# The sample units' last product with pairs of V heads as its stationary operand

## The chip, the cores and the metric

The kernel runs on one core of one Trainium2 chip. The metric is the device time of one execution in microseconds. A profile of one further execution, taken by the hardware profiler, shows what each engine did: PE is the matrix engine (PEld its loads of the stationary operand), DVE the vector engine, ACT the scalar engine, POOL GpSimd, SP the engine that issues most DMAs.

## What is computed

The reference is one inference step of a streaming encoder of two layers (width 1024, 16 heads of 64, 4 K/V heads, MLP of 4096), for a prompt of 1024 new frames and for 8 running streams ("sample") of 16 new frames each, which attend to 128 cached positions beside their own. Layer 0 has windowed attention with a distance penalty and sinks, layer 1 chunked attention with a learned bias; K and V of layer 1 come from a projection of the residual after layer 0. The part that the change touches is the sample attention, in both layers:

```python
def attend(q, k, v, bias, sink):
    qg = q.reshape(b, tq, N_KV_HEADS, GROUP, HEAD_DIM)
    s = jnp.einsum('bqhgd,bkhd->bhgqk', qg, k).astype(jnp.float32) * (HEAD_DIM ** -0.5)
    s = s + bias.reshape(N_KV_HEADS, GROUP, tq, -1)
    # softmax over keys, in layer 0 with the sink in its denominator -> p
    o = jnp.einsum('bhgqk,bkhd->bqhgd', p.astype(v.dtype), v)
    return o.reshape(b, tq, N_HEADS * HEAD_DIM)

k_all = jnp.concatenate([cache_k_a[i], ks_], axis=1)   # cache (8, 128, 4, 64), new (8, 16, 4, 64)
v_all = jnp.concatenate([cache_v_a[i], vs_], axis=1)
as_ = attend(qs, k_all, v_all, alibi_bias(pos_s, kpos_a, slopes), sink_a[i])
```

## The kernel before

Tokens are tiles of 128: eight of the prompt and one that holds all 8 x 16 sample tokens. Each layer is a phase of attention (about 25 to 400 us of the span in layer 0, 1130 to 1605 in layer 1), the output projection, the MLP's up part and its down part. Most products take fp32 data split in a high and a low part of type fp32r and are three products of 128x128 by 512 (lines 250 to 252, 205 to 207, 800 to 802).

In the attention phase, a loop over 16 pairs of steps does the prompt's attention, for one tile and one K/V head at a time: scores (L423, L475), softmax, transposes of the probabilities (L362), their split (`pth` by ACT at L154, `ptl` by DVE at L160), the product with V (L370 and L371, called from `V` in `attention`). Other work is put between these steps by tables (`at`, `shift`, `plan`): projections of later tiles, the output projection, and the steps of one *sample unit* at a time.

A sample unit (function `unit`, 16 in each layer) takes one K/V head `j` and two of the 8 streams (`bp`): 4 query heads x 2 streams x 16 tokens are its 128 rows. It is a generator with four places at which other work comes between. It

- loads the cached K (`kc`) and V (`vc`) of that head and those two streams, 128 positions each, and the queries (`qu`) by DMAs that SP issues;
- makes K's split and its transpose (L622, `ps_utr`, copied to `kb` by ACT at L623) and the scores (L627, `ps_us`);
- makes the softmax with ACT and DVE, with the normalized probabilities in `p` and those of the new tokens in `pn`;
- transposes them in three 128x128 pieces (L652 to L654, `ps_utp`), which ACT copies to `pts` (L656);
- makes the last product (L660 to L662): stationary are `vc` for each of the two streams and then `v8`, the new tokens' V, 64 columns each; moving is `pts`, 128 columns. All are plain fp32, not fp32r;
- copies the result's blocks to `so` with two ACT copies (L665) and stores it (L666).

The pool of the unit's tiles has one buffer for each, so the next unit's `vc` is loaded when this one's product is done. The result tile `ps_uo` comes from the PSUM tag `g`, shared with the transposes and the products with V.

The order of instructions on each engine is not the order of the code: the framework's planner simulates a timeline with costs of its own, takes ranks into account (tables `rank`, `rank_s` and so on, and `WO_PRIO`), and writes a fixed order for each engine at build time. An instruction of another shape has another cost in that simulation, and the order around it can come out differently.

Of the kernel before, what the change touches and what calls it, by code (L numbers as in the profile page):

```python
# [10 lines left out]
F32 = mybir.dt.float32  # L11
# [7 lines left out]
P = 128  # L19
# [8 lines left out]
HD = 64  # L28
# [92 lines left out]
class Build:  # L121
# [461 lines left out]
    @ranked_steps  # L583
    def unit(self, up, small, layer, bp, j, v8, gq8, cache_k, cache_v):
        nc = self.nc
        kc = up.tile([P, 2, HD], F32, tag="kc", name="kc")
        nc.sync.dma_start(kc, cache_k[2 * bp : 2 * bp + 2, :, j, :].rearrange("b k d -> k b d"))
        vc = up.tile([P, 2, HD], F32, tag="vc", name="vc")
        nc.sync.dma_start(vc, cache_v[2 * bp : 2 * bp + 2, :, j, :].rearrange("b k d -> k b d"))
        qu = up.tile([P, 2, P], F32R, tag="qu", name="qu")  # L590
        qd = self.qT8d[layer][j][:, bp * P : bp * P + P]
        nc.sync.dma_start(qu[:, 0].bitcast(F32), qd)
        nc.sync.dma_start(qu[0:64, 1].bitcast(F32), qd[64:128])
        nc.sync.dma_start(qu[64:128, 1].bitcast(F32), qd[0:64])
        kb = up.tile([P, 288], F32R, tag="kb", name="kb")
        nc.sync.dma_start(
            kb[:, 256:288].bitcast(F32), self.kT8d[layer][:, j, bp * 32 : bp * 32 + 32]
        )
        if layer == 0:
            bias = self.cst[:, C_SA : C_SA + 288]  # L600
        else:
            bias = up.tile([P, 288], F32, tag="ub", name="ub")
            nc.sync.dma_start(bias, self.biasSd[j])
        kp = kc
        self.eng("c").tensor_tensor(kp, kc, gq8.unsqueeze(1).to_broadcast([P, 2, HD]), ALU.mult)
        if "p" in self.engs:
            yield
            a, b = slice(0, 64), slice(64, 128)
            pt = self.psum("u", [P, P], "ps_utr")
            nc.tensor.transpose(pt, kp.rearrange("p b d -> p (b d)"), self.ident)  # L610
            self.split(kb[a, 0:P], kb[b, 0:P], pt[a])
            self.split(kb[b, P : 2 * P], kb[a, P : 2 * P], pt[b])
        else:
            ks = up.tile([P, 2, P], F32R, tag="uks", name="uks")
            nc.gpsimd.tensor_copy(ks[:, :, 0:HD], kp)
            self.eng("u").tensor_tensor(
                ks[:, :, HD:P], kp, ks[:, :, 0:HD].bitcast(F32), ALU.subtract
            )
            yield
            pt = self.psum("u", [P, 2, P], "ps_utr")  # L620
            for b in range(2):
                nc.tensor.matmul(pt[:, b, :], ks[:, b, :], self.identr, start=True, stop=True)  # L622
            nc.scalar.copy(kb[:, 0:256], pt.rearrange("p b k -> p (b k)"))  # L623
        yield
        s = self.psum("u", [P, 288], "ps_us")
        for v in range(2):
            nc.tensor.matmul(s, qu[:, v], kb, start=(v == 0), stop=(v == 1))  # L627
        mn = small.tile([P, 1], F32, tag="smn", name="smn")
        pn = up.tile([P, P], F32, tag="pn", name="pn")
        nc.gpsimd.memset(pn, 0.0)  # L630
        p = up.tile([P, 288], F32, tag="sp", name="sp") if layer == 0 else bias
        l = small.tile([P, 1], F32, tag="sl", name="sl")
        if layer == 0:
            nc.vector.tensor_tensor_reduce(
                s, s, bias, 1.0, self.susink[:, j : j + 1], ALU.add, ALU.min, mn
            )
            nm = small.tile([P, 1], F32, tag="snm", name="snm")
            nc.vector.tensor_tensor(nm, mn, self.cst[:, C_SLS + j : C_SLS + j + 1], ALU.mult)
            nc.scalar.activation(
                p, s, AF.Exp, bias=nm, scale=self.nslope[:, j : j + 1], accum_out=l  # L640
            )
            li = self.sink_norm(small, nm, self.ssink[:, j : j + 1], l, 1)
        else:
            nc.vector.tensor_tensor_reduce(s, s, bias, 1.0, BIG, ALU.add, ALU.min, mn)
            nc.scalar.activation(p, s, AF.Exp, bias=mn, scale=-1.0, accum_out=l)
            li = small.tile([P, 1], F32, tag="sli", name="sli")
            self.mark = nc.vector.reciprocal(li, l)
        nc.scalar.activation(p[:, 0:256], p[:, 0:256], AF.Copy, scale=li)
        nc.scalar.activation(pn[:, bp * 32 : bp * 32 + 32], p[:, 256:288], AF.Copy, scale=li)
        yield  # L650
        pt2 = self.psum("u", [P, 3, P], "ps_utp")
        nc.tensor.transpose(pt2[:, 0, :], p[:, 0:128], self.ident)  # L652
        nc.tensor.transpose(pt2[:, 1, :], p[:, 128:256], self.ident)
        nc.tensor.transpose(pt2[:, 2, :], pn, self.ident)  # L654
        pts = up.tile([P, 3, P], F32, tag="pts", name="pts")
        nc.scalar.copy(pts, pt2)  # L656
        yield
        po = self.psum("u", [64, 2, 2, 32], "ps_uo")
        pof = po.rearrange("p a b q -> p (a b q)")
        nc.tensor.matmul(pof, vc[:, 0, :], pts[:, 0, :], start=True, stop=False)  # L660
        nc.tensor.matmul(pof, vc[:, 1, :], pts[:, 1, :], start=False, stop=False)
        nc.tensor.matmul(pof, v8[:, j * HD : j * HD + HD], pts[:, 2, :], start=False, stop=True)  # L662
        so = up.tile([P, 2, 32], F32, tag="so", name="so")
        for par in range(2):
            nc.scalar.copy(so[par * 64 : par * 64 + 64], po[:, :, par, :])  # L665
        nc.sync.dma_start(  # L666
            self.oTd[layer][j // 2][ST][:, 0, 2 * (j % 2) : 2 * (j % 2) + 2, bp * 32 : bp * 32 + 32], so
        )
# [1364 lines left out]
```

## Time and profile before

| | |
|---|---|
| median of 3 runs | 2330.3 us (2327.54 to 2332.09) |
| the profiled execution | 2332.31 us, span 2330.5 us |
| granted clock of the matrix engine, mean | 0.993 |
| instructions on PE | 11429 products, as many loads |
| the unit's last products | 192 of them (32 units x 3 x 2 passes) |
| the unit's V loads | 32, 64 KB each |

In the profile's rows, a product reads "128*64 128x128": 128 rows by 64 columns of the stationary operand, then the moving data, 128 partitions by 128 elements. A product's end is modelled, and records of products that follow each other overlap; so the distance from start to start says what one costs, rather than its length. "idle before" is the time in which the engine (PEld: the load) had nothing running ahead of the instruction, with the names of those whose end released it.

### The profile page before, as it was taken

How to read it: one execution, taken by the hardware profiler on the slowest of the kernel's cores; microseconds unless marked ns; L12 is line 12 of the kernel's file. 1: busy time of each engine (PE TensorE's matmuls, PEld its weight loads, DVE VectorE, ACT ScalarE, POOL GpSimd, SP SyncE). 2: the span in 40 equal slices, each digit the busy share in tenths (PEclk: the TensorE clock that was granted, in tenths of full speed). 3: DMA queues.
4: the chain of work that ended last, by engine and by line, in shares of the span. 5: the costliest groups of instructions: out<-in, count | busy, mean ns of one | idle time of the engine just before them, and what ended most of it. 6: DMA issues, size and time to landing. Idle time of an engine off the chain costs nothing.

```text
span 2330.5 us, 33408 instructions
## 1 busy us (share of the span) xinstructions
PE 2273.0 (98%) x11429; PEld 1899.7 (82%) x11429; DVE 1705.2 (73%) x3072; ACT 1330.4 (57%) x2684; POOL 635.5 (27%) x952
## 2 busy tenths in 40 slices
PE   8999999999999999999999999998999999999999
PEld 6787877888888888788788788887888888888887
DVE  6878776856656587898678877777665665778987
ACT  3777665655555555444377666665655555565443
POOL 4333332322222211002443434344222132110011
PEclk9999999999999999999999999999999999999999
DMA  7335566244433688548744656555244343977567
GB/s 274 115 113 160 170 196 204 101 135 145 146 126 127 215 233 196 203 146 199 220 150 115 189 164 182 172 170 176 95 142 139 122 155 113 285 206 197 181 165 199
DMA packets 226219, 392.70 MB, mean 169 GB/s; under 512 B 51592, under 2 KB 125776, under 8 KB 225936
## 3 DMA queue, kind: packets, MB, share of 16 engines
q1 hardware_dynamic: 188320, 283.58, 38.2%
q0 software_dynamic: 36432, 102.26, 16.1%
q10 hardware_dynamic: 1296, 4.72, 0.5%
q8 instruction: 90, 1.47, 0.3%
q14 instruction: 81, 0.66, 0.1%
HBM read 237.10 MB, written 157.15 MB: 169 GB/s over the span
## 4 chain that ended last, share of the span: by engine, by line
PE 83%; DVE 7%; DMA 5%; ACT 3%; issue 1%; SPq 0%; POOL 0%; ACTq 0%; DVEq 0%; POOLq 0%
PE ps_c L800 8%; PE ps_c L801 8%; PE ps_c L802 8%; PE ps_x L800 5%; PE ps_x L802 5%; PE ps_x L801 5%; PE ps_mm L250 4%; PE ps_mm L252 4%; PE ps_mm L251 4%; PE ps_y L802 2%; PE ps_y L801 2%; PE ps_y L800 2%; PE ps_tr L362 2%; PE ps_mm L205 2%; PE ps_mm L206 2%; PE ps_mm L207 2%
## 5 line engine op out<-in xcount | busy, mean ns | idle before, releaser
L800 PE MATMUL ps_c<-w,a 128*128 128x512 f32 x960 | 374.0, 390 | 3.0 <-ACT o L1236 2.0
L801 PE MATMUL ps_c<-w,a 128*128 128x512 f32 x960 | 373.7, 389 | 0.8 <-DVE w L160 0.8
L802 PE MATMUL ps_c<-w,a 128*128 128x512 f32 x960 | 373.5, 389 | 0.0
L988 POOL DMA_DIRECT2D hd<-h x272 | 148.8, 550 | 573.3 <-ACT h L890 377.3
L800 PEld LDWEIGHTS ps_c<-w,a 128*128 128x128 f32 x960 | 180.2, 188 | 42.4 <-ACT o L1236 3.3
L801 PEld LDWEIGHTS ps_c<-w,a 128*128 128x128 f32 x960 | 180.2, 188 | 38.5 <-DVE w L160 1.5
L802 PEld LDWEIGHTS ps_c<-w,a 128*128 128x128 f32 x960 | 180.2, 188 | 37.5
L154 ACT CAST a<-a 128x1536 fp32r<-128x1536 f32 x80 | 118.7, 1483 | 153.2 <-DMA a<-hd 153.0
L250 PE MATMUL ps_mm<-w,hh 128*128 128x512 f32 x432 | 174.4, 405 | 12.1 <-ACT hh L154 5.3
L252 PE MATMUL ps_mm<-w,hl 128*128 128x512 f32 x432 | 173.5, 402 | 1.9 <-DVE hl L160 1.9
L251 PE MATMUL ps_mm<-w,hh 128*128 128x512 f32 x432 | 172.3, 399 | 0.1
L160 DVE TENSOR_TENSOR a<-a 128x1536 fp32r<-128x1536 f32 x80 | 140.2, 1752 | 35.1 <-ACT a L154 34.8
L154 ACT CAST w<-ru 128x512 fp32r<-128x512 f32 (+1 forms) x160 | 110.0, 708 | 89.6 <-PE ps_y L801 32.0
L800 PE MATMUL ps_x<-sx,w 128*128 128x512 f32 (+1 forms) x408 | 158.2, 388 | 0.3 <-ACT w L154 0.3
L154 ACT CAST w<-s 128x2048 fp32r<-128x2048 f32 x56 | 107.1, 1912 | 86.6 <-DVE s L1137 74.9
L802 PE MATMUL ps_x<-sx,w 128*128 128x512 f32 (+1 forms) x408 | 154.8, 379 | 0.9 <-DVE w L160 0.9
L801 PE MATMUL ps_x<-sx,w 128*128 128x512 f32 (+1 forms) x408 | 154.6, 379 | 0.0
L160 DVE TENSOR_TENSOR w<-s,w 128x2048 fp32r<-128x2048 f32 x56 | 128.2, 2288 | 33.9 <-ACT w L154 33.9
L1253 POOL DMA_DIRECT2D xp<-o x28 | 36.2, 1294 | 407.6 <-ACT o L1236 386.2
L160 DVE TENSOR_TENSOR ptl<-ps_tr,pth 128x512 fp32r<-128x512 f32 x180 | 122.0, 684 | 22.5 <-ACT pth L154 20.5
L160 DVE TENSOR_TENSOR w<-ru,w 128x512 fp32r<-128x512 f32 (+1 forms) x160 | 127.3, 798 | 14.4 <-ACT w L154 14.3
L889 ACT ACTIVATE h<-h 128x512 f32<-128x512 f32 (+1 forms) x102 | 62.0, 607 | 117.8 <-DVE h L940 93.7
(273 smaller groups left out, 6120.8 us busy)
## 6 DMA issues: line engine op xcount, KB each, us to landing
a<-hd SPq DMA_DIRECT2D x80, 768.0 KB, 5.5
hd<-h POOLq DMA_DIRECT2D x272, 192.0 KB, 2.5
ru<-in_w_up SPq DMA_DIRECT2D x64, 512.0 KB, 3.8
r<-in_w_down SPq DMA_DIRECT2D x32, 1024.0 KB, 9.6
xp<-o POOLq DMA_DIRECT2D x28, 768.0 KB, 9.5
o<-oTd SPq DMA_DIRECT2D x50, 256.0 KB, 4.0
x<-xp SPq DMA_DIRECT2D x23, 512.0 KB, 5.4
xp<-xo SPq DMA_DIRECT2D x18, 512.0 KB, 3.1
```

The source lines that it names most:

```text
L154: a = nc.scalar.copy(hi, src)
L160: return a, e.tensor_tensor(lo, src, hi.bitcast(F32), ALU.subtract)
L205: nc.tensor.matmul(ps, oh[:, k, :], w[:, 0, k, nn], start=(k == 0), stop=False)
L206: nc.tensor.matmul(ps, oh[:, k, :], w[:, 1, k, nn], start=False, stop=False)
L250: nc.tensor.matmul(ps, a, w[:, 0, k, :], start=(k == 0), stop=False)
L251: nc.tensor.matmul(ps, a, w[:, 1, k, :], start=False, stop=False)
L252: self.lp = nc.tensor.matmul(ps, b, w[:, 0, k, :], start=False, stop=(k == KC - 1))
L800: a = mm(ps, ah, bh, start=first, stop=False, skip_group_check=True)
L801: mm(ps, ah, bl, start=False, stop=False, skip_group_check=True)
L802: return a, mm(ps, al, bh, start=False, stop=last, skip_group_check=True)
L889: a = nc.scalar.activation(t, src, AF.Relu)
L988: return lambda p, z: self.nc.gpsimd.dma_start(self.hd[c // 4][:, p, c % 4], z)
```

## The change

The cached V is loaded for the pair of heads that `j` belongs to (heads 0 and 1, or 2 and 3), so `vc` has 128 columns for each stream instead of 64, and the load brings 128 KB instead of 64. The three products take all 128 columns, and `v8` likewise those of the pair. The result has 128 partitions instead of 64: the lower 64 for the pair's first head and the upper 64 for its second. The two copies read only the half that belongs to `j`; the other half is not used. The number of instructions is the same.

```diff
-        vc = up.tile([P, 2, HD], F32, tag="vc", name="vc")
-        nc.sync.dma_start(vc, cache_v[2 * bp : 2 * bp + 2, :, j, :].rearrange("b k d -> k b d"))
+        jj = slice(j // 2 * 2, j // 2 * 2 + 2)
+        vc = up.tile([P, 2, 2, HD], F32, tag="vc", name="vc")
+        nc.sync.dma_start(vc, cache_v[2 * bp : 2 * bp + 2, :, jj, :].rearrange("b k j d -> k b j d"))
...
-        po = self.psum("u", [64, 2, 2, 32], "ps_uo")
+        po = self.psum("u", [P, 2, 2, 32], "ps_uo")
         pof = po.rearrange("p a b q -> p (a b q)")
-        nc.tensor.matmul(pof, vc[:, 0, :], pts[:, 0, :], start=True, stop=False)
-        nc.tensor.matmul(pof, vc[:, 1, :], pts[:, 1, :], start=False, stop=False)
-        nc.tensor.matmul(pof, v8[:, j * HD : j * HD + HD], pts[:, 2, :], start=False, stop=True)
+        v2 = v8.rearrange("p (j d) -> p j d", d=HD)
+        nc.tensor.matmul(pof, vc[:, 0], pts[:, 0, :], start=True, stop=False)
+        nc.tensor.matmul(pof, vc[:, 1], pts[:, 1, :], start=False, stop=False)
+        nc.tensor.matmul(pof, v2[:, jj], pts[:, 2, :], start=False, stop=True)
+        own = slice(j % 2 * HD, j % 2 * HD + HD)
         so = up.tile([P, 2, 32], F32, tag="so", name="so")
         for par in range(2):
-            nc.scalar.copy(so[par * 64 : par * 64 + 64], po[:, :, par, :])
+            nc.scalar.copy(so[par * 64 : par * 64 + 64], po[own, :, par, :])
```

Lines behind the edit have numbers that are 1 to 3 higher in the changed kernel (L660 becomes L662, L652 becomes L653).

In most places the order stays and only the shape differs. On PE, around the unit's product at about 1495 us of the span (layer 1; `ps_pv` is the prompt's product with V, `ps_tr` a transpose of its probabilities, `ps_sf` scores), before:

```order
L362 MATMUL ps_tr<-identr,p 128x128 x4
L370 MATMUL ps_pv<-pth,VS 128x512
L660 MATMUL ps_uo<-pts,vc 64x128
L661 MATMUL ps_uo<-pts,vc 64x128
L371 MATMUL ps_pv<-ptl,VS 128x512
L662 MATMUL ps_uo<-pts,v_11164 64x128
L362 MATMUL ps_tr<-identr,p 128x128 x4
L475 MATMUL ps_sf<-KT,qT 128x384 x4
```

and now:

```order
L362 MATMUL ps_tr<-identr,p 128x128 x4
L370 MATMUL ps_pv<-pth,VS 128x512
L662 MATMUL ps_uo<-pts,vc 128x128
L663 MATMUL ps_uo<-pts,vc 128x128
L371 MATMUL ps_pv<-ptl,VS 128x512
L664 MATMUL ps_uo<-pts,v_11164 128x128
L362 MATMUL ps_tr<-identr,p 128x128 x4
L475 MATMUL ps_sf<-KT,qT 128x384 x4
```

Nothing moved there: the same product L371 still stands between the second and the third product of the unit, and the three rows of the unit have 128 columns.

Between about 184 and 243 us, in layer 0, the order differs on PE, ACT, DVE and POOL. PE around a unit's scores (`ps_us`) at about 206 us, before (the products L250 to L252 go on for some 25 rows from here; `ps_q` transposes queries):

```order
L370 MATMUL ps_pv<-pth,VS 128x512
L622 MATMUL ps_utr<-identr,uks 128x128 x2
L295 MATMUL ps_q<-identr,qr 128x128 x4
L627 MATMUL ps_us<-kb,qu 128x288 x2
L250 MATMUL ps_mm<-w,hh 128x512
L251 MATMUL ps_mm<-w,hh 128x512
L252 MATMUL ps_mm<-w,hl 128x512
```

and now:

```order
L370 MATMUL ps_pv<-pth,VS 128x512
L623 MATMUL ps_utr<-identr,uks 128x128 x2
L295 MATMUL ps_q<-identr,qr 128x128 x4
L628 MATMUL ps_us<-kb,qu 128x288 x2
L371 MATMUL ps_pv<-ptl,VS 128x512
L370 MATMUL ps_pv<-pth,VS 128x512
L362 MATMUL ps_tr<-identr,p 128x128 x4
L250 MATMUL ps_mm<-w,hh 128x512
L251 MATMUL ps_mm<-w,hh 128x512
```

Two products with V (L371, L370) and four transposes (L362) now stand right behind the unit's scores; before, they came behind the products L250 to L252.

ACT at the same place (`oh` is the high part of an attention output that a DMA brought, `kb` the unit's K, `so` the result of the unit before), before:

```order
L154 CAST w<-raw 128x1024
L665 COPY so<-ps_uo 64x64 x2
L154 CAST pth<-ps_tr 128x512 x2
L154 CAST oh<-o 128x512
L623 CAST kb<-ps_utr 128x256
L261 COPY qr<-ps_mm 128x512
L154 CAST qT<-ps_q 64x4x128
L438 ACTIVATE p,l<-ps_s,nm 128x256 x2
```

and now:

```order
L154 CAST w<-raw 128x1024
L668 COPY so<-ps_uo 64x64 x2
L154 CAST pth<-ps_tr 128x512
L154 CAST oh<-o 128x512
L154 CAST pth<-ps_tr 128x512
L624 CAST kb<-ps_utr 128x256
L438 ACTIVATE p,l<-ps_s,nm 128x256 x2
L261 COPY qr<-ps_mm 128x512
```

Of two casts of `pth`, the second now stands behind `oh`, and two exponentials (L438) come ahead of `qr`. SP's order differs in a few rows at the same time (a query store and a load of `kc` among them). Behind 243 us, PE's order is that of before but for two swaps, of one pair of products with V at about 381 us and of three products in the MLP at about 1646 us.

## The prediction

> **What bounds the kernel now.** I read the page first, then the groups of PE by line and shape, then short timelines around one last product of a sample unit, then the chain of waits.
>
> ```profile
> span 2330.5 us, 33408 instructions
> PE 2273.0 (98%) x11429; PEld 1899.7 (82%) x11429; DVE 1705.2 (73%) x3072; ACT 1330.4 (57%) x2684; POOL 635.5 (27%) x952
> PE 83%; DVE 7%; DMA 5%; ACT 3%; issue 1%; SPq 0%; POOL 0%; ACTq 0%; DVEq 0%; POOLq 0%
> ```
>
> PE sets the pace: 83% of the chain that ended last is PE. A busy share of 98% does not say that PE streams all that time: the records overlap, and stalls shorter than a record are covered by it. So I looked for such stalls in the lines that the change touches.
>
> ```profile
> L660 PE MATMUL ps_uo<-pts,vc 128*64 128x128 f32 x64 | 13.8, 298 | 0.8 <-ACT pts L656 0.8
> L660 PEld LDWEIGHTS ps_uo<-pts,vc 128*64 128x64 f32 x64 | 6.1, 134 | 10.0 <-issue 4.2 <-ACT pts L656 1.2 <-ACT p L438 1.1
> L661 PEld LDWEIGHTS ps_uo<-pts,vc 128*64 128x64 f32 x64 | 7.9, 137 | 0.0
> L423 PEld LDWEIGHTS ps_s<-KT,qT 128*128 128x128 f32 x256 | 36.7, 189 | 6.3 <-ACT p L438 2.6 <-DVE qT L160 0.8 <-ACT qr L261 0.4
> ```
>
> There are 32 units; each product has 64 records, so one fp32 product is two passes, and a unit issues six passes, each with its own load. The first load (L660) has 10.0 us of load idle before it, 0.31 us for each unit, and its named releasers explain little of it. What happens there shows in a timeline (start, length), here of PE around one unit between two 512-wide products, with the loads that begin it and follow it:
>
> ```profile
> 257.17 0.39 PE L207 MATMUL ps_mm<-w,ol 128*128 128x512 f32 x1
> 257.48 0.43 PE L660 MATMUL ps_uo<-pts,vc 128*64 128x128 f32 x2
> 257.75 0.38 PE L661 MATMUL ps_uo<-pts,vc 128*64 128x128 f32 x2
> 257.97 0.38 PE L662 MATMUL ps_uo<-pts,v 128*64 128x128 f32 x2
> 258.28 0.50 PE L370 MATMUL ps_pv<-pth,VS 128*128 128x512 f32 x1
> 258.62 0.39 PE L371 MATMUL ps_pv<-ptl,VS 128*128 128x512 f32 x1
> 257.48 0.19 PEld L660 LDWEIGHTS ps_uo<-pts,vc 128*64 128x64 f32 x2 [0.36 <-ACT p L438]
> 258.28 0.19 PEld L370 LDWEIGHTS ps_pv<-pth,VS 128*128 128x128 f32 x1 [0.17 <-issue]
> ```
>
> And the same neighbours around the three 128-column transposes of a unit:
>
> ```profile
> 1598.28 0.39 PE L370 MATMUL ps_pv<-pth,VS 128*128 128x512 f32 x1
> 1598.51 0.27 PE L652 MATMUL ps_utp<-identr,ub 128*128 128x128 f32 x1
> 1598.62 0.27 PE L653 MATMUL ps_utp<-identr,ub 128*128 128x128 f32 x1
> 1598.72 0.27 PE L654 MATMUL ps_utp<-identr,pn 128*128 128x128 f32 x1
> 1598.75 0.48 PE L371 MATMUL ps_pv<-ptl,VS 128*128 128x512 f32 x1
> 1599.07 0.39 PE L370 MATMUL ps_pv<-pth,VS 128*128 128x512 f32 x1
> 1598.28 0.14 PEld L652 LDWEIGHTS ps_utp<-identr,ub 128*128 128x128 f32 x1
> ```
>
> With 128 columns the load of L652 starts with the product ahead of it (1598.28), and the switch costs nothing: 0.23 us later the transpose runs. With 64 columns the load waits 0.31 us (257.17 to 257.48) until the product ahead is over, and the next 128-column load waits again until L662 is over (0.17 us idle). On both sides of the 64-column group the array runs empty. The rule of the Trainium skill that bears on this is in "TensorEngine Tiling (Array Packing)", Tiling Modes, Key Properties: "Mode switching requires drain". By that rule, whose drain the rows agree with, 128 columns take both stalls away.
>
> **The change part by part.** Removed: the two drains. From the product ahead to the second product behind, the 64-column unit takes 258.62 - 257.17 = 1.45 us. With 128 columns the same stretch is 0.23 (entry, 1598.28 to 1598.51), five steps between six passes, and 0.35 (exit, 1598.72 to 1599.07).
>
> The step. It is 0.108 us between L652 and L654, where a load lasts 0.14 us. A full load that is no transpose lasts 189 ns (L423), and there the step is 0.47/4 = 0.118 us, at 256 columns of moving data:
>
> ```profile
> 93.11 0.64 PE L423 MATMUL ps_s<-KT,qT 128*128 128x256 f32 x4
> 93.58 0.40 PE L252 MATMUL ps_mm<-w,hl 128*128 128x512 f32 x1
> ```
>
> So five steps cost 0.54 to 0.59 us, and a unit 1.12 to 1.17: it saves 0.28 to 0.33 us. I take 0.28, as the plain load of 128 columns is nearest to L423. "TensorE: Matmul & The Clock Gate", LDWEIGHTS (loading the stationary operand), of the Trainium skill speaks against the change: a load takes its columns over 1.2 GHz, so by my estimate from it the 192 loads would grow by 53 ns each, 10.2 us if none were hidden. The rows 137 and 189 ns agree with that growth; that it hides is read from the step above.
>
> Before a transpose the exit is shorter:
>
> ```profile
> 240.75 0.38 PE L662 MATMUL ps_uo<-pts,v 128*64 128x128 f32 x2
> 241.06 0.88 PE L362 MATMUL ps_tr<-identr,p 128*128 128x128 f32 x6
> 1495.09 0.38 PE L661 MATMUL ps_uo<-pts,vc 128*64 128x128 f32 x2
> 1495.40 0.50 PE L371 MATMUL ps_pv<-ptl,VS 128*128 128x512 f32 x1
> 1495.83 0.43 PE L662 MATMUL ps_uo<-pts,v 128*64 128x128 f32 x2
> 1496.19 0.66 PE L362 MATMUL ps_tr<-identr,p 128*128 128x128 f32 x4
> ```
>
> L662 to its successor takes 0.31 us there, in which two passes of 0.108 lie, and the first transpose then waits for its own load; I put the saving at 0.045 us less than above, 0.235 us. By the timelines 13 units are followed by a transpose and 19 by something wider: 19 x 0.28 + 13 x 0.235 = 8.4 us (10.0 us at the short step). In two units, of which the rows from 1495.09 are one, a 512-wide product (L371) stands inside the group, so both drains are paid twice: L661 to L662 takes 0.74 us where 0.22 and a product of 0.23 would be 0.45, some 0.3 each, 0.6 in all. Eight units wait for their data longer than the drain; the entry gains nothing there (0.08 us each, 0.6 in all) and their first load, 52 ns longer, may be bare (0.4). PE's gain: 8.4 + 0.6 - 0.6 = 8.4 us, bounds 8.0 and 10.6.
>
> What of it is on the path: in the chain of waits the product group appears in 25 of the 32 units, the first two and the last of them:
>
> ```profile
> 95.59 0.36 PE ps_uo L660 x2
> 117.85 0.36 PE ps_uo L660 x2
> 1588.48 0.36 PE ps_uo L660 x2
> ```
>
> 8.4 x 25/32 = 6.6 us. The other seven stand where ACT, DVE or a DMA set the time.
>
> Moved: with another shape the planner puts the work of layer 0's attention in another order between about 184 and 243 us; behind that PE's order is the same but for two small swaps. In that stretch the chain of waits leaves PE, and in parts of it the clock was halved, as in the second row:
>
> ```profile
> 178.00:232.00 54.00, 49.67 (x258) 39.71 (x259) 47.14 (x142) 42.80 (x120) 18.16 (x35) 0.94 0.54 161
> 205.40:208.90 3.50, 3.17 (x8) 2.66 (x9) 3.01 (x7) 3.50 (x12) 0.00 (x0) 0.52 0.19 63
> 204.79 0.62 ACT L154 CAST oh<-o 128x512 fp32r<-128x512 f32 x1 [1.95 <-DMA o<-oTd]
> 205.73 0.85 PE L627 MATMUL ps_us<-kb,qu 128*128 128x288 f32 x2 [2.19 <-ACT kb L623]
> ```
>
> (The fields behind the window's length are busy time of PE, PEld, DVE, ACT and POOL, then clock, DMA share, GB/s.) ACT waits 1.95 us for a DMA with oh, its kb stands behind, and PE behind kb. In the new order one of two casts of pth stands behind oh too, and PE asks for it right behind ps_us, ahead of some 25 products that covered it. The cast costs kb about 0.5 us there. On the other side the transposes that stood behind those products come 5 us sooner, which is good for DVE and ACT. A half-clock stretch of 3.5 us costs 1.7 us; one more or one less is possible. I put the reorder at 0, bounds -4 and +4 us.
>
> Added: 64 KB per unit of V that is not used. The load's buffer is free as soon as L661 is done, and it is read a unit later, about 20 us (95.59 to 117.85 for the first two).
>
> ```profile
> vc<-in_cache_v_a SPq DMA_DIRECT2D x16, 64.0 KB, 2.5
> vc<-in_cache_v_b SPq DMA_DIRECT2D x16, 64.0 KB, 3.5
> L665 ACT COPY so<-ps_uo 64x64 f32<-64x64 f32 x64 | 13.1, 205 | 16.1 <-PE ps_uo L662 15.7
> ```
>
> Even twice 3.5 us is covered three times by that; SP issues the same number of transfers. Were the cover gone, a unit would wait up to 3.5 us. The copies on ACT (L665) keep 64x64 elements and only read another half of the partitions: 0.
>
> The sum. The profiled execution took 2332.3 us (span 2330.5, the rest around it), 2.0 above the median of the runs shown. 2332.3 - 6.6 = 2325.7, or **2323.7 us** beside the median.
>
> **The rivals.**
>
> *The drain belongs to the two-pass fp32 product, not to the 64 columns.* In this trace the two cannot be told apart: the only rows with 64 columns are also the only ones with two passes. Against it speaks that inside the group six passes of it follow each other without a drain, and that the transposes, fp32 too, enter and leave freely. Then the drains stay and the bare first load is 52 ns longer, the five steps 0 to 0.045: 32 x 0.052 to 0.097 = 1.7 to 3.1 us on PE, 1.3 to 2.4 on the path: 2332. This would be the case that the change doesn't do what it says.
>
> *PE gains, but the rest takes it back.* DVE, ACT and the DMAs hold 15% of the chain, and DVE is busy 47.14 of 54 us in the stretch from 178. If there the gain before 243 us is lost, and what layer 0 gains behind it waits for DMAs, the 14 units of layer 1 on the chain are left: 14 x 0.26 = 3.6 us, 2326.7, within what can be told from no change.
>
> *The new order stalls.* One mechanism: behind ps_us at about 206 us PE waits for pth and ptl, which ACT makes only after its wait for oh; PE idles, and its clock halves. Price: 2 us a step for the four units up to 243 us, and half clock for three stretches, 8 + 5 = 13 us, less 6.6: 2337. It decides only from 11 us of loss on. Against it: before, the same engines had PE busy in 49.67 of 54 us there.
>
> **How the numbers follow.** My forecast 0.62, the fp32 rival 0.14, the gain taken back 0.17, the stall 0.07. The likeliest case alone spans 2318 to 2328: 10.6 us all on the path with a lucky order below, the order's 4 us above. Range 2317 to 2332, which takes in the two rivals in between and leaves out the stall. A measurement of this kernel tells 0.2%, 4.7 us, from no change: faster means below 2325.6. Faster: 0.80 of the forecast and a third of the gain taken back, 0.55. Same: 0.12 + 0.11 + 0.12 = 0.35. Slower: the stall, a little of the fp32 rival and of a bad order, 0.10.
>
> **What would show it.** The load idle before the first product falls from 10.0 us to under 3, and the timeline shows its load starting with the product ahead: the drain is the columns'. Loads of the group last about 189 ns with steps of 0.11 to 0.12; steps of 0.2 would mean that a full fp32 load does not hide. Layer 1 (1200 to 1605 us), whose order is unchanged, must be some 3 to 4 us shorter; if it is not, the theory of the drain or of the path is wrong. Layer 0's stretch from 178 to 243 us tells what the order did. A longer wait of PE for ptl or kb there would make the prediction wrong on the slow side.

## The result, and the profile after

| | before | after |
|---|---|---|
| median, runs side by side | 2331.61 us (6 runs, 2327.54 to 2336.88) | 2319.99 us (6 runs, 2317.25 to 2324.45) |
| the profiled execution | 2332.31 us, span 2330.5 us | 2321.66 us, span 2319.9 us |

The ratio is 0.9956, with a 95% interval from 0.9944 to 0.9967: between 7.7 and 13.1 us of 2331.6, 10.3 in the middle. The forecast was 6.6 us. Two later comparisons of the same two kernels on other chips (in the experiments) gave 0.9972 and 0.9965, 6.5 and 8.2 us. Over all runs whose granted clock is known one by one the means are 2329.7 us (73 runs of before) and 2322.3 (24 of the change), 7.4 apart. So the change is faster, by 7 to 8 us, and the first comparison stands high.

The page of the changed kernel, in the lines that answer those shown of before (span, busy time of the engines, the chain of waits by engine):

```profile
span 2319.9 us, 33409 instructions
PE 2260.6 (97%) x11429; PEld 1898.7 (82%) x11429; DVE 1707.1 (74%) x3072; ACT 1330.5 (57%) x2684; POOL 634.7 (27%) x952
PE 78%; DMA 7%; DVE 6%; issue 4%; ACT 3%; POOL 1%; SPq 0%; ACTq 0%; DVEq 0%; POOLq 0%
```

PE still sets the pace. PE's busy time fell by 12.4 us, though it executes as many products, and the time of its loads hardly moved, though 192 of them became longer. The groups of the last product by line and shape (count, then busy time and mean ns of one, then the idle time ahead of them):

```profile
L662 PE MATMUL ps_uo<-pts,vc 128*128 128x128 f32 x64 | 12.5, 277 | 1.0 <-ACT pts L657 1.0
L662 PEld LDWEIGHTS ps_uo<-pts,vc 128*128 128x128 f32 x64 | 11.5, 188 | 3.1 <-ACT pts L657 1.4
L663 PEld LDWEIGHTS ps_uo<-pts,vc 128*128 128x128 f32 x64 | 9.7, 192 | 0.0
L664 PEld LDWEIGHTS ps_uo<-pts,v 128*128 128x128 f32 x64 | 9.9, 192 | 0.1
```

The first load's idle time fell from 10.0 to 3.1 us. The loads went from 134 and 137 ns to 188 and 192. The same neighbours as in the prediction's timeline, PE first and then the two loads:

```profile
257.25 0.39 PE L207 MATMUL ps_mm<-w,ol 128*128 128x512 f32 x1
257.48 0.38 PE L662 MATMUL ps_uo<-pts,vc 128*128 128x128 f32 x2
257.70 0.39 PE L663 MATMUL ps_uo<-pts,vc 128*128 128x128 f32 x2
257.92 0.39 PE L664 MATMUL ps_uo<-pts,v 128*128 128x128 f32 x2
258.06 0.48 PE L370 MATMUL ps_pv<-pth,VS 128*128 128x512 f32 x1
258.38 0.39 PE L371 MATMUL ps_pv<-ptl,VS 128*128 128x512 f32 x1
257.25 0.41 PEld L662 LDWEIGHTS ps_uo<-pts,vc 128*128 128x128 f32 x2
258.03 0.19 PEld L370 LDWEIGHTS ps_pv<-pth,VS 128*128 128x128 f32 x1
```

The first load starts with the product ahead of it, at 257.25, and L370's load starts at 258.03, while the unit's last product still runs. The stretch from the product ahead to the second product behind is 258.38 - 257.25 = 1.13 us, where it was 1.45. Passes follow each other at 0.22/2 = 0.11 us (553 ns for five steps), so the longer load hides. And the same view of the changed kernel where a product stands inside the group, and a transpose behind it:

```profile
1485.51 0.47 PE L370 MATMUL ps_pv<-pth,VS 128*128 128x512 f32 x1
1485.83 0.38 PE L662 MATMUL ps_uo<-pts,vc 128*128 128x128 f32 x2
1486.04 0.39 PE L663 MATMUL ps_uo<-pts,vc 128*128 128x128 f32 x2
1486.19 0.47 PE L371 MATMUL ps_pv<-ptl,VS 128*128 128x512 f32 x1
1486.50 0.38 PE L664 MATMUL ps_uo<-pts,v 128*128 128x128 f32 x2
1486.72 0.60 PE L362 MATMUL ps_tr<-identr,p 128*128 128x128 f32 x4
```

L663 to L664 takes 0.46 us (0.74 before) and L664 to the transpose 0.22 (0.36 before).

### The profile page after: what moved, and what is told of

Same layout as the page of the kernel before. It is cut to its first block, busy times and chain, and to the rows that moved or that the text cites. A ratio compares the mean times of both kernels' runs of the same rounds, so it can differ in the third digit from the quotient of the medians.

```text
span 2319.9 us, 33409 instructions
## 1 busy us (share of the span) xinstructions
PE 2260.6 (97%) x11429; PEld 1898.7 (82%) x11429; DVE 1707.1 (74%) x3072; ACT 1330.5 (57%) x2684; POOL 634.7 (27%) x952
## 4 chain that ended last, share of the span: by engine, by line
PE 78%; DMA 7%; DVE 6%; issue 4%; ACT 3%; POOL 1%; SPq 0%; ACTq 0%; DVEq 0%; POOLq 0%
PE ps_c L803 7%; PE ps_c L804 7%; PE ps_c L805 7%; PE ps_x L803 5%; PE ps_x L805 5%; PE ps_x L804 5%; PE ps_mm L250 4%; PE ps_mm L252 4%; PE ps_mm L251 4%; PE ps_y L805 2%; PE ps_y L804 2%; PE ps_y L803 2%; PE ps_tr L362 2%; PE ps_mm L205 1%; PE ps_mm L206 1%
## 5 line engine op out<-in xcount | busy, mean ns | idle before, releaser
L250 PE MATMUL ps_mm<-w,hh 128*128 128x512 f32 x432 | 174.1, 404 | 10.9 <-ACT hh L154 5.3
L252 PE MATMUL ps_mm<-w,hl 128*128 128x512 f32 x432 | 172.8, 400 | 1.4 <-DVE hl L160 1.4
L1256 POOL DMA_DIRECT2D xp<-o x28 | 36.2, 1294 | 407.6 <-ACT o L1239 386.4
```

What stands on the lines that cost most here:

```text
L250: nc.tensor.matmul(ps, a, w[:, 0, k, :], start=(k == 0), stop=False)
L252: self.lp = nc.tensor.matmul(ps, b, w[:, 0, k, :], start=False, stop=(k == KC - 1))
L1256: nc.gpsimd.dma_start(dst, z, accum_op=ALU.add)
```

## Experiments

Three questions: whether the gain is that of the columns alone (and what in 64 columns makes the drain), what the new order in layer 0 does, and why the first comparison gave more than the products explain. Times are medians, ratios are against the kernel before, run beside it on the same chip. Edits are shown against the changed kernel where nothing else is said.

**The load alone.** The load takes the pair of heads, the products stay at 64 columns.

```diff
-        po = self.psum("u", [P, 2, 2, 32], "ps_uo")
+        po = self.psum("u", [64, 2, 2, 32], "ps_uo")
...
-        nc.tensor.matmul(pof, vc[:, 0], pts[:, 0, :], start=True, stop=False)
-        nc.tensor.matmul(pof, vc[:, 1], pts[:, 1, :], start=False, stop=False)
-        nc.tensor.matmul(pof, v2[:, jj], pts[:, 2, :], start=False, stop=True)
-        own = slice(j % 2 * HD, j % 2 * HD + HD)
+        nc.tensor.matmul(pof, vc[:, 0, j % 2], pts[:, 0, :], start=True, stop=False)
+        nc.tensor.matmul(pof, vc[:, 1, j % 2], pts[:, 1, :], start=False, stop=False)
+        nc.tensor.matmul(pof, v2[:, j], pts[:, 2, :], start=False, stop=True)
+        own = slice(0, HD)
```

> The wide load alone: vc is loaded for the pair of heads (128 KB), but the three products keep 64 columns, of the own head. The order on every engine is that of before. Theory (the gain is the two drains around a 64-column group): the drains stay, about 10 us of load idle before the first product, entry 0.31 us and exit 0.20 us behind the last product's start; time within 0.2% of before (2327 to 2336). Rival (larger pieces of the V load help the DMAs and so the rest): at least a third of the 11.6 us, 3 to 5 us faster.

Measured: 2328.8 us against 2329.64, ratio 0.9996 (0.9985 to 1.0008). The drains are all there; the row of the first load is that of the kernel before:

```profile
L662 PEld LDWEIGHTS ps_uo<-pts,vc 128*64 128x64 f32 x64 | 6.1, 134 | 10.0 <-issue 4.2 <-ACT pts L657 1.2 <-ACT p L438 1.1
```

The wider load changes nothing that can be measured. What follows belongs to the products.

**One layer at a time.** The whole change in one layer, 64 columns in the other.

```diff
-        jj = slice(j // 2 * 2, j // 2 * 2 + 2)
+        wide = layer == 1
+        jj = slice(j // 2 * 2, j // 2 * 2 + 2) if wide else slice(j, j + 1)
...
-        po = self.psum("u", [P, 2, 2, 32], "ps_uo")
+        po = self.psum("u", [P if wide else 64, 2, 2, 32], "ps_uo")
...
-        own = slice(j % 2 * HD, j % 2 * HD + HD)
+        own = slice(j % 2 * HD, j % 2 * HD + HD) if wide else slice(0, HD)
```

> Pairs of heads in layer 1 only; layer 0 as before, and the order on every engine is that of before. Theory: 16 units at 0.28 us and two split groups, 4.5 to 5 us from the drains, all behind 1200 us; what is above it (the whole change took 7.9 us between the units' first and last in layer 1) comes from a wait of PE for hh near 1305 us and the half-clock stretch behind it. If that comes with the change, 7 to 8 us faster and no half-clock stretch near 1308 us; if it was luck of one execution, 4 to 5 us faster and the stretch is there in some executions.

Measured: 2323.41 us, ratio 0.9973 (0.9961 to 0.9985), 6.3 us, between the two cases of the expectation. Its profile has no half clock near 1308 us, but that of the load alone, which keeps the drains, has none there either; so the missing stretch doesn't come with the change.

The other layer has the same edit with `wide = layer == 0`, and the new order.

> Pairs of heads in layer 0 only; the order is that of the whole change. Theory: 16 units at 0.25 us, 4 us, less what the other order between 184 and 243 us costs (the whole change lost 1.7 us between the fifth and the eighth unit): 2 to 3 us faster by the end of layer 0's attention. Rival (the order costs nothing, the loss was an accident of one profile): 4 us faster or more.

Measured: 2325.84 us, ratio 0.9982 (0.9972 to 0.9992), 4.2 us, in time the rival's case. Each layer gains, and both together give 10.5 with an uncertainty of about 4; they don't contradict 7 to 8. Both sets also ran at a higher mean granted clock than before beside them (0.9951 and 0.9953 against 0.9945), which by the table of clocks below goes with 1 to 2 us of each.

**The old order with the wide products.** All units are wide but one, unit 4 of layer 0; the planner then gives the order of before, and the stretch between 184 and 243 us is not moved.

```diff
+        wide = layer == 1 or 4 * j + bp not in (4,)
```

> The whole change but for the fifth unit of layer 0 (at 178 us), which keeps 64 columns: then the planner gives the order of before but for one swap of two products at 381 us and one DMA. Theory (the new order costs 1.5 to 3 us): 13 to 15 us faster than before, 1 to 3 us faster than the whole change, although one unit's 0.28 us is given back. Rival (the order is free): 0.3 us slower than the whole change, 11 us faster than before.

Measured: 2322.13 us, ratio 0.9961 (0.9945 to 0.9976): 9.1 us, where 13 to 15 were expected, and 11 if the order is free. The same kernel was run once more, on a third chip, with the whole change beside it:

> The kernel of e4 (fifth unit of layer 0 narrow, order of before), this time beside the whole change on one chip. Theory (the new order costs 2 to 3 us at full clock, as e3's and e4's times at full clock and the units' places read): 2 to 3 us below the whole change at full clock, and 2 us in time where both lose the same clock. Rival (the order is free): 0.3 us above it at full clock.

> The whole change beside e9, on the same chip. Theory: 6 to 7 us below before at full clock, 0.9955 to 0.9975 of before in time; its place against e9 as that one's expectation says.

Measured there: 2321.3 us with the old order, ratio 0.9971 (0.9959 to 0.9982), and 2322.26 us for the whole change, ratio 0.9965 (0.9952 to 0.9978). I had thought that the new order costs 1 to 3 us, from the one profile after, in which the stretch is longer than before. In time the two orders are the same, within these intervals. At equal clock they are not, as the expectation had it; the table of clocks below shows that, and what the profiles show of the stretch is told ahead of it.

**The whole change again**, on the second chip, beside the three that follow.

> The whole change once more, beside the others of this chip. Theory (the drains give 7 us at full clock, the rest of the 10 us are fewer half-clock stretches): 0.9956 of before again within 0.001, and time less the clock lost to half-clock stretches 7 us below that of before. If the stretches were luck, 0.997 of before, with the same clock as before's runs.

Measured: 2322.15 us against 2330.72, ratio 0.9972 (0.9955 to 0.9988). That is the second case of the expectation: 0.997, at the clock of before's runs (means 0.9942 and 0.9940).

**A busy PE during a wait.** In layer 1's output projection, sixteen 512-wide products whose result nobody reads are put ahead of a piece that waits near 1605 us, to keep the clock up there.

```diff
+                if layer == 1 and t == 7:
+                    with self.lift(-3000):
+                        ps = self.psum("m", [P, 512], "ps_dummy")
+                        for _ in range(16):
+                            nc.tensor.matmul(ps, self.identr, wo[:, 0, 0, 0:512], start=True, stop=True)
```

> The whole change, with 16 products of 128x128 by 512 that nobody reads put on PE in the output projection of layer 1, where PE waits 4.2 us for a DMA (about 1598 to 1602 us); the output is the same. Theory (a half-clock stretch follows an idle PE): the stretch of 6.8 us behind that wait is gone, 3.4 us faster than the whole change of the same chip, less what the added products stand in the way (0 to 1 us). Rival (the stretch has another cause, or the wait is unchanged and only covered): the clock is halved there as before, and the time is that of the whole change or up to 1 us more.

Measured: 2325.2 us, ratio 0.9975 (0.9962 to 0.9987): no gain over the whole change (2322.15 beside it), where 3.4 us were expected. The windows behind the wait (length, busy time of PE, PEld, DVE, ACT, POOL, then the clock, DMA share, GB/s), of the whole change run beside it:

```profile
1602.00:1609.00 7.00, 5.86 (x16) 4.43 (x17) 6.66 (x12) 4.98 (x10) 1.11 (x2) 0.57 0.57 188
```

and of this kernel, at the same place and some 20 us later:

```profile
1605.00:1612.00 7.00, 6.73 (x38) 5.20 (x37) 5.03 (x10) 6.65 (x13) 0.56 (x1) 1.00 0.69 225
...
1628.00:1636.00 8.00, 6.49 (x31) 5.94 (x32) 8.00 (x14) 4.09 (x9) 5.24 (x5) 0.57 0.23 66
```

Its timeline of PE at the later place (start, length, in brackets the idle time ahead and what ended it):

```profile
1628.46 1.75 PE L749 MATMUL ps_n<-identr,s 128*128 128x128 f32 x8 [3.00 <-DVE mms L688]
```

The half clock behind the wait is gone, 0.57 to 1.00. The ten other profiles with the fp32 product all have a half-clock stretch there, behind a wait of 3.0 to 4.5 us, so busy work does keep the clock. But the planner also moved what comes behind: PE waits 3.00 us at 1628, and runs at half clock there. Seven of those ten profiles have a second half-clock stretch some 25 us behind the first as well, so this one can't be put down to the added products alone. The kernel differs in its order behind 1606 us too, so its time doesn't price the stretch.

**96 columns.** For the first head of each pair, the products take 96 columns, for the second all 128.

```diff
-        po = self.psum("u", [P, 2, 2, 32], "ps_uo")
+        mc = 96 if j % 2 == 0 else P
+        po = self.psum("u", [mc, 2, 2, 32], "ps_uo")
...
-        nc.tensor.matmul(pof, v2[:, jj], pts[:, 2, :], start=False, stop=True)
+        nc.tensor.matmul(pof, v8[:, j0 : j0 + mc], pts[:, 2, :], start=False, stop=True)
```

> The whole change, but the units of even heads take 96 of the 128 columns (the own 64 and half of the other head). Theory A (the array changes its mode at 64 columns, and 96 need the mode of 128): no drain in any unit, load idle before the first product about 3 us, time of the whole change. Theory B (any number of columns but 128 drains): 16 of 32 units drain, load idle about 6 us, 3 to 4 us slower than the whole change.

Measured: 2321.3 us, ratio 0.9962 (0.9945 to 0.998), the same as the whole change. Its groups of the first product's loads, by shape:

```profile
L663 PEld LDWEIGHTS ps_uo<-pts,vc 128*96 128x96 f32 x32 | 5.1, 162 | 1.3
L663 PEld LDWEIGHTS ps_uo<-pts,vc 128*128 128x128 f32 x32 | 5.6, 189 | 2.1 <-ACT pts L657 1.4
```

and its timeline of PE around a unit of 96 columns:

```profile
254.91 0.39 PE L207 MATMUL ps_mm<-w,ol 128*128 128x512 f32 x1
255.13 0.38 PE L663 MATMUL ps_uo<-pts,vc 128*96 128x128 f32 x2
255.35 0.38 PE L664 MATMUL ps_uo<-pts,vc 128*96 128x128 f32 x2
255.57 0.38 PE L665 MATMUL ps_uo<-pts,v 128*96 128x128 f32 x2
255.71 0.48 PE L370 MATMUL ps_pv<-pth,VS 128*128 128x512 f32 x1
256.02 0.40 PE L371 MATMUL ps_pv<-ptl,VS 128*128 128x512 f32 x1
```

256.02 - 254.91 = 1.11 us: no drain at 96 columns. So it is not "fewer than 128" that drains, and a load of another length (162 ns) does not bring a drain by itself. Where between 64 and 96 columns it begins was not tested. The drain of 64 columns agrees with the Trainium skill, "TensorEngine Tiling (Array Packing)", Tiling Modes, Available Configurations, which lists 128x64 as a mode of its own and nothing with 96 columns. That a plain product of 64 columns runs in that mode is inferred.

**64 columns in one pass.** The prediction could not tell 64 columns from two passes. This is the kernel before (the edit is shown against it) with the last product in bf16: GpSimd converts V to `vb`, and `pts` is written as bf16, so that V and the probabilities keep only the bits of bf16 in this product.

```diff
+        vb = up.tile([P, 3, HD], mybir.dt.bfloat16, tag="vb", name="vb")
+        nc.gpsimd.tensor_copy(vb[:, 0:2], vc)
+        nc.gpsimd.tensor_copy(vb[:, 2], v8[:, j * HD : j * HD + HD])
...
-        pts = up.tile([P, 3, P], F32, tag="pts", name="pts")
+        pts = up.tile([P, 3, P], mybir.dt.bfloat16, tag="pts", name="pts")
...
-        nc.tensor.matmul(pof, vc[:, 0, :], pts[:, 0, :], start=True, stop=False)
+        nc.tensor.matmul(pof, vb[:, 0], pts[:, 0, :], start=True, stop=False)
...
```

> Before, with the unit's last product in bf16: 64 columns as before, but one pass for each product instead of two (GpSimd converts V, ACT writes pts in bf16, so V and the probabilities lose their low bits). The order changes on all engines, so only the timeline around the products counts. Theory (the 64 columns drain): the first load still starts 0.31 us behind a 512-wide product ahead, and the next load waits for the last product. Rival (it takes two-pass fp32 with 64 columns): the first load starts with the product ahead, as with 128 columns.

Measured: 2349.4 us in the one run. The planner put the whole program in another order, so the time says nothing on the product; the timeline of PE and of two loads does:

```profile
253.35 0.39 PE L207 MATMUL ps_mm<-w,ol 128*128 128x512 f32 x1
253.67 0.24 PE L663 MATMUL ps_uo<-pts,vb 128*64 128x128 bf16 x1
253.75 0.22 PE L664 MATMUL ps_uo<-pts,vb 128*64 128x128 bf16 x1
253.81 0.22 PE L665 MATMUL ps_uo<-pts,vb 128*64 128x128 bf16 x1
253.95 0.50 PE L370 MATMUL ps_pv<-pth,VS 128*128 128x512 f32 x1
254.29 0.39 PE L371 MATMUL ps_pv<-ptl,VS 128*128 128x512 f32 x1
253.67 0.11 PEld L663 LDWEIGHTS <-vb 128*64 128x64 bf16 x1 [0.36 <-issue]
253.95 0.19 PEld L370 LDWEIGHTS ps_pv<-pth,VS 128*128 128x128 f32 x1
```

One pass, half the bytes, and the entry is 253.67 - 253.35 = 0.32 us with the load behind the product's end, as with fp32 at 64 columns (0.31). At the exit L370's load starts 0.14 us after L665's start, not with it. The drain is that of the 64 columns; the number of passes has nothing to do with it. With 96 columns in two passes and no drain, both sides of that rival are tested.

**The stretch with the new order.** Nearly all of the moved work lies between unit 4's product and unit 8's, in layer 0. The window between those two starts (columns as above), in the profile of before:

```profile
178.29:257.48 79.19, 74.86 (x395) 60.83 (x394) 63.79 (x205) 58.17 (x169) 27.61 (x53) 0.96 0.55 172
```

of the old order with wide products, on the third chip:

```profile
179.29:258.45 79.16, 73.47 (x395) 60.31 (x395) 63.63 (x205) 57.91 (x169) 27.57 (x53) 0.98 0.55 173
```

of after:

```profile
177.07:257.48 80.41, 73.73 (x396) 60.35 (x395) 65.80 (x208) 58.75 (x169) 29.33 (x53) 0.98 0.56 169
```

and of the whole change on the third chip:

```profile
177.66:254.95 77.29, 72.38 (x395) 59.08 (x395) 64.59 (x208) 58.80 (x169) 29.31 (x53) 1.00 0.58 178
```

The same kernel takes 80.41 us in one execution and 77.29 in another. PE's wait for `kb` ahead of the unit's scores goes with it. The row of the timeline, in after:

```profile
205.35 0.53 PE L628 MATMUL ps_us<-kb,qu 128*128 128x288 f32 x2 [2.38 <-ACT kb L624]
```

and in the whole change on the third chip:

```profile
204.17 0.53 PE L628 MATMUL ps_us<-kb,qu 128*128 128x288 f32 x2 [0.59 <-ACT kb L624]
```

Over eleven profiles (all but that of the bf16 product, whose order is its own): with the old order (before, the load alone, layer 1 alone, and twice the old order with wide products) the wait is 2.0 to 2.7 us every time, half clock comes with it, and the stretch takes 79.1 to 79.9. With the new order, three profiles have a wait of 1.5 to 2.5 us with half clock beside it and a stretch of 80.0 to 80.8 (after, the whole change again, and the busy PE); the other three wait 0.3 to 0.9 us, have no half clock behind it, and take 77.3 to 78.0. So by these profiles the new order is better there in half of the executions, by 1 to 2 us, and worse by some 1 us in the other half. Why `kb` is late in some executions was not followed further.

**Where the first comparison's extra came from.** Each run's mean granted clock is known, to 0.001. Mean time (and number of runs) by that clock, all comparisons together; for the six runs of before in the first comparison only the times are at hand, so they are left out:

```
granted clock   before        load alone   old order, wide   whole change   whole - before
0.993           2332.3 (16)   2331.1 (3)   2323.0 (5)        2324.4 (3)     -7.9
0.994           2330.8 (13)   2329.7 (2)   2320.2 (3)        2323.2 (8)     -7.6
0.995           2328.5 (21)   2327.4 (3)   2318.7 (5)        2321.5 (5)     -7.0
0.996           2326.2 (14)   2325.8 (1)   2319.1 (1)        2319.7 (6)     -6.5
```

Three things stand in it. Within one kernel 0.001 of clock goes with about 2 us, so a good part of the runs' spread is the clock's. At equal clock the change gives 6.5 to 7.9 us. And the old order with wide products gives more, 7.1 to 10.6 us, 0.6 to 3.0 below the whole change: what its second expectation said, 2 to 3 us. Its 18 runs had a lower mean clock, 0.9937 against 0.9946 of the whole change's 24, which goes with some 2 us, and so the times are the same. The new order seems to cost some 2 us and to get them back by a higher clock. The groups are small, and no run shows where these 2 us lie.

The first comparison's six runs of the changed kernel had a mean of 0.9955, all of its 24 runs 0.9946, the 73 of before in the later comparisons 0.9943: some 2 us of the 10.3 are a higher clock, which did not come again on the other two chips. That would be the larger part of the extra, if the six runs of before at its side had their usual clock; the rest lies within its interval.

That such waits and stretches are an accident of the execution shows in layer 1, at PE's wait for `hh` near 1305 us. The timeline of the kernel before:

```profile
1307.74 0.52 PE L250 MATMUL ps_mm<-w,hh 128*128 128x512 f32 x1 [3.39 <-DMA hh<-hTd]
```

its window there, with the clock at 0.76:

```profile
1305.00:1312.00 7.00, 4.26 (x16) 3.96 (x17) 5.87 (x18) 3.21 (x9) 3.33 (x4) 0.76 0.87 275
```

and the timeline of the load alone, which keeps the drains:

```profile
1308.24 0.47 PE L250 MATMUL ps_mm<-w,hh 128*128 128x512 f32 x1 [1.80 <-DMA hh<-hTd]
```

Between the units on both sides of it (19 and 20) the profile of before takes 43.05 us, the load alone 39.88 and the profile after 39.85: 3.2 us that have nothing to do with the products. They sit in the one profile of before; in the whole change on the third chip they stand again, with a wait of 3.42 us and 42.8 us between the units.

## Why the prediction was right

The forecast was 2323.7 us, 6.6 less than before; the six runs gave 2319.99, inside the range, and over three comparisons the gain is 7 to 8 us. Step by step:

- **The drains are those of the 64 columns, and 128 takes them away.** Right. The first load's idle time is 3.1 us ("under 3" was short by the 1.4 that `pts` makes it wait), both loads start with the product ahead, and the experiments with 96 columns and with one pass exclude the other reading. The fp32 rival, at 2332, is refuted.
- **The unit's stretch.** Entry 0.23 us was measured as 0.23. The step was put at 0.118 between bounds of 0.108 and 0.118, from the loads nearest in length; it is 0.111 (0.553 for five instead of 0.59). The exit, 258.38 less the last pass's start at 258.03, is 0.35, as put. So a unit saves 0.32 us where a wide product follows, not 0.28: this is a term that was mis-sized. Before transposes the saving was put at 0.235, and it is 0.28: a group ahead of one takes 0.89 us now and took 1.11, and the four transposes behind it take 0.60 where they took 0.66. The split group: 1486.72 - 1485.51 = 1.21 us, which took 1.78 before, and 0.06 more for its transposes; 0.63, where 0.235 + 0.3 was taken.
- **The sum.** Added up unit by unit over both traces, from the product ahead to the second one behind, PE takes 9.9 us less, where 8.4 was forecast. The term of -0.6 for eight units that wait for data was close to nothing: the entry near 1253 us, for one, fell from 0.41 to 0.31 us, as much as where no data is waited for. Only two units, near 200 and 373 us of before, save next to nothing (-0.2 and 0.1). The chain of after still has the product in 25 of the 32 units, and they hold 8.4 of the 9.9 us, against 7 to 8 measured. That the path takes just this share isn't shown: at equal clock the old order, with 31 of the 32 units wide, gains 7.1 to 10.6.
- **Layer 1, "some 3 to 4 us shorter".** About right, though the two profiles alone say otherwise: from its first unit's product to its last one's, before takes 392.5 us and after 384.6. 3.2 of these 7.9 are the accident at 1305 us. Taken over the profiles with 64 columns in layer 1 (392.5, 389.7, 388.2) and with more (384.6, 385.3, 386.0, 386.4, 389.5, 386.7, 383.0, 383.6), the means differ by 4.5 us, and the three of the one kind spread over nearly as much.
- **The load of 128 KB at no cost.** Right: 0.9996 for it alone. It lands in 3.6 and 3.9 us, where 64 KB took 2.5 and 3.5.

```profile
vc<-in_cache_v_a SPq DMA_DIRECT2D x16, 128.0 KB, 3.6
vc<-in_cache_v_b SPq DMA_DIRECT2D x16, 128.0 KB, 3.9
```

- **The copies on ACT at no cost.** Right: 64 copies of 206 ns, 205 before. That their source begins at partition 64 in half of the units makes no difference.
- **The reorder at 0, between -4 and +4.** Right in time, and in part by luck: the old order with wide products runs as fast as the new one, within the intervals, but at equal clock it is some 2 us ahead, and the new order's higher clock, which was not forecast, makes up for it. The reason given, that the cast of `pth` costs `kb` 0.5 us, was wrong as a rule: the wait for `kb` is shorter with the new order in four of six profiles. The rival of the new order, in which PE idles behind `ps_us` for `pth` and `ptl`, did not come: the products L371 and L370 follow `ps_us` after 0.37 and 0.22 us in the profile after, neither waits, and only the `kb` wait ahead remains (its row, from 205.35, is shown above).

```profile
205.72 0.39 PE L371 MATMUL ps_pv<-ptl,VS 128*128 128x512 f32 x1
205.94 0.48 PE L370 MATMUL ps_pv<-pth,VS 128*128 128x512 f32 x1
```

- **The gain taken back**, 2326.7: refuted. Layer 0 gains by itself (0.9982, 4.2 us, of which some 1.6 go with a higher clock), and the gain is kept through the waits for DMAs.
- **Half clock, "one more or one less is possible", priced at 1.7 us.** Right in kind. Some 2 us of the six runs' 10.3 go with their higher clock, more than any one term of PE's sum was off by (each under 1 us).

What stays open: why a given wait of 1 to 4 us is followed by half clock in one execution and not in another. The Trainium skill, "TensorE: Matmul & The Clock Gate", Part 1, says that the gate watches a window of 3.4 us that runs freely, and that the moment at which the clock changes depends on where in the window the work begins. The stretches here last about 3.4 us, or twice that, which agrees. In the profile after, the clock is at half from 206.1 to 209.5, from 339.2 to 342.6 and from 1602.2 to 1609.0 us, and these times lie whole multiples of 3.41 us apart, which agrees too; whether the place of a wait between such times decides was not followed. Open too is where the new order loses its 2 us at equal clock, and whether it is by this order that the clock is higher.

## What to carry to other kernels

A stationary operand of 64 columns between products of 128 costs this kernel about 0.3 us for each group, which the busy share hides and the load's idle time shows: look at whether a load starts with the product ahead of it. Widening the operand with columns that nobody reads cost nothing here, where PE's loads hide behind its passes, and 96 columns did as well as 128. Where a gain is a few tenths of a per cent, compare runs at equal granted clock as well as by their times, since an order can change the clock too, and read a stretch from more than one profile before a wait in it is priced.

## What the runs showed of the hardware

- 96 columns don't drain: entry 0.22 us and a whole stretch of 1.11 us, against 0.31 and 1.45 for 64.
- bf16 in one pass drains at 64 columns just as fp32 in two does: 0.32 us at the entry.
- An fp32 load lasts 134 to 137 ns for 64 columns, 162 for 96, 188 to 192 for 128; the step between passes with 128 moving columns stays at 0.109 to 0.111 us from 96 to 128 columns.
- A PE wait of 1.5 us or more near 206 us came with half clock each time (eight profiles of eight), one under 0.9 us never (three of three).
